# HGRN sample tokens as weights in four 32-column array tiles, states as moving operand, turned back by a selection product

## The chip, the cores and the metric

The kernel runs on one core of one Trainium2 chip. The metric is device time in microseconds (us). The kernel before takes 1646.91 us, the median of three runs (1646.46 to 1647.82).

The names used for engines: PE is TensorE, the matmul array, and PEld its weight loads; DVE is VectorE, ACT ScalarE, POOL GpSimd, and SP SyncE, which here only issues DMAs.

## The reference, cut to what matters

One layer of a hybrid decoder runs on 256 prompt tokens and on 64 sample tokens (8 sequences of 8 tokens). The input projection feeds three groups: RWKV-7 (12 heads), HGRN2 (6 heads, each with a 128 x 128 state) and RG-LRU. Then come an output projection and a gated MLP. The change is in HGRN2:

```python
def step(S, inp):
    q_c, k_c, v_c, lf_c = inp
    b = jnp.cumsum(lf_c, axis=1)
    o_inter = jnp.einsum('bthk,bhkv->bthv', q_c * jnp.exp(b), S)
    dec = jnp.exp(jnp.where(causal, b[:, :, None] - b[:, None, :], -jnp.inf))
    A = jnp.einsum('bthk,btshk,bshk->btsh', q_c, dec, k_c)
    o = o_inter + jnp.einsum('btsh,bshv->bthv', A, v_c)
    ...
    return S, o
...
o = rms_norm(o, lp['hgrn_norm_w'].reshape(HGRN_HEADS, HGRN_HEAD_DIM)).reshape(B, T, HGRN_WIDTH)
o = o * jax.nn.silu(g.astype(f32))
```

For a sample sequence, `o_inter` is the product of its 8 tokens (query times `exp(b)`) with that sequence's own state `S`. There are 8 such states in a head.

## The kernel before

All 320 tokens stand as columns, features on partitions. Weights are streamed in chunks of 512 KB (`raw`, three buffers, a DMA on SP's queue at L167). Each chunk is split into a rounded part `wh` (ACT, L173) and the rest `wl` (DVE, L174). A chunk then is 24 matmuls of 320 moving columns: L198 and L199 in turn, eight of each, with `wh`, and then eight L205 with `wl`. This weight stream is nearly the whole of PE's work.

Everything else runs in chains, which are Python generators. Each chain yields a delay (`L_EV`, `L_SUB` and others); a clock counts weight matmuls and chain steps, and after every four L198/L199 pairs, and after a chunk, the chains that are due go on by a step. The Tile scheduler then makes the final order of each engine from the recorded instructions, and may move them further. The order is so set by these delays and the scheduler together.

In the first third of the kernel six pairs of RWKV heads and six HGRN heads alternate. Two places matter here.

*The inverse triangles of an RWKV pair.* A block of coefficients `mt1` is stored to memory by SP (L568, `dn`) and read back as 16 x 16 blocks (L569, `n16`). Fifteen steps of two DVE operations (L573 and L575) build their inverses `u16`. SP stores them (L576, `du`) and reads them as a whole (L577, `Us`). On PE, L648 transposes `Us`; ACT copies the result (L649), and L665 and what follows merge the triangles into larger ones. The chain has `yield L_SUB` ahead of L648.

*The output of an HGRN head.* L960 to L962 make the prompt's output from `vt` (values with tokens on partitions) and `at` (the attention matrix). L963 makes the sample tokens' part inside a sequence, with 64 rows. L965 runs eight matmuls: the weights are a state `s0` (128 x 128, called `hs` in the trace), and 8 columns of `eb` (query times `exp(b)`) move. The sum's square goes through a matmul with ones (L971), and ACT and DVE make the normalised output from it (L973 to L977). L990/L991 and L998 make the new states, which L1000 adds on DVE.

Of the kernel before, what the change touches and what calls it, by code (L numbers as in the profile page):

```python
# [10 lines left out]
F32 = mybir.dt.float32  # L11
F32R = mybir.dt.float32r
U8 = mybir.dt.uint8
AF = mybir.ActivationFunctionType
ALU = mybir.AluOpType
AX = mybir.AxisListType

P = 128
D = 2048
NK = D // P  # L20
TP = 256
SB, ST = 8, 8
TS = SB * ST
T = TP + TS
# [28 lines left out]
_n = 0  # L53
for _name, _w in (
    ("ident", 128), ("ones", 128), ("bones", 128), ("bswap", 128), 
    ("psw", 128), ("eye2", 64), ("bmx", 4), ("bm4", 4),
):
    CST[_name] = (_n, _w)
    _n += _w
# [7 lines left out]
def kernel(ctx: ExitStack, tc: tile.TileContext, i: dict, o: dict):  # L67
    nc = tc.nc
    V, S, G, PE, SY = nc.vector, nc.scalar, nc.gpsimd, nc.tensor, nc.sync
# [7 lines left out]
    def aux_r():  # L77
        return aux_p.tile([P, 512], F32, tag="aux_r", name="aux_r", bufs=NAUX_R)

    def aux_h():  # L80
        return aux_p.tile([P, 512], F32, tag="aux_h", name="aux_h", bufs=6 - NAUX_R)
# [107 lines left out]
    def gemm(pieces, xh, xl, k0=0, first=True, last=True, ps=None):  # L189
        if ps is None:  # L190
            ps = acc_p.tile([P, 512], F32, tag="acc", name="acc")
        for c, kc in enumerate(pieces):
            prefetch()
            wh, wl = splits.pop(state["used"])
            state["used"] += 1
            for k in range(kc):
                st = first and c == 0 and k == 0
                PE.matmul(ps[:, :T], wh[:, k, :], xh[k0 + k], start=st, stop=False)  # L198
                PE.matmul(ps[:, :T], wh[:, k, :], xl[k0 + k], start=False, stop=False)  # L199
                state["clock"] += 2 * GEMM_COST  # L200
                if k % 4 == 3:
                    tick()
            for k in range(kc):
                en = last and c == len(pieces) - 1 and k == kc - 1
                PE.matmul(ps[:, :T], wl[:, k, :], xh[k0 + k], start=False, stop=en)  # L205
                state["clock"] += GEMM_COST
            k0 += kc
            prefetch()
            tick()
        return ps  # L210
# [9 lines left out]
    def split_tiles(k):  # L220
        return (xp.tile([P, T], F32R, tag=f"xh{k}", name=f"xh{k}"),
                xp.tile([P, T], F32R, tag=f"xl{k}", name=f"xl{k}"))
# [18 lines left out]
    mp = mix.enter_context(tc.tile_pool(name="mixconst", bufs=1))  # L241
    rp = mix.enter_context(tc.tile_pool(name="mixrot", bufs=1))
# [25 lines left out]
    for k in range(NK):  # L268
        if k % 4 == 0:
            split_weights(2 * (k // 8), slice(k % 8, k % 8 + 4))  # L270
        a, b = split_tiles(k)
# [52 lines left out]
    def free(*owners):  # L324
        for owner in owners:
            owner[0] = True

    def ht(name, w=T):
        return rp.tile([P, w], F32, tag="hc", name=name, bufs=BHC)
# [90 lines left out]
    def flat(ap):  # L420
        return ap.rearrange("p a b -> p (a b)")
# [103 lines left out]
    def rwkv_chunks(p, lw, box):  # L525
# [117 lines left out]
        for e in range(2):  # L643
            S.copy(flat(rq[:, 2 * e:2 * e + 2, :]), pss[e][:, 0:256])
        yield L_SUB
        ps = aux_r()
# [175 lines left out]
    def projected(name):  # L822
        ps = gemm(W_CHUNKS, xh, xl)
        t, owner = gt_(name)
        V.tensor_tensor(t, ps[:, :T], rstd, op=ALU.mult)
        return t, owner

    def hgrn_head(n):
        box = {"q": projected("hq")}
        box["f"] = projected("hf")  # L830
        spawn("h", hgrn_steps(n, box))
        box["v"] = projected("hv")
        box["g"] = projected("hg")

    def hgrn_steps(n, box):
        (q, q_own), (f, f_own) = box["q"], box["f"]
        s0 = []
# [4 lines left out]
        b = ht("b", T)  # L842
# [10 lines left out]
        at = ht("at", T)  # L853
# [32 lines left out]
        e, f = ht("e", T), ht("f", T)  # L886
# [13 lines left out]
        while h <= P:  # L900
# [14 lines left out]
            else:  # L915
                ps = aux_h()
# [11 lines left out]
        S.activation(x[:, TP:T], x[:, TP:T], AF.Exp)  # L928
        kd = ht("kd", T)
        V.tensor_tensor(kd, k, x, op=ALU.mult)  # L930
        eb = rp.tile([P, TS], F32, tag="eb", name="eb", bufs=1)
        S.activation(eb, b[:, TP:T], AF.Exp)
        V.tensor_tensor(eb, q[:, TP:T], eb, op=ALU.mult)

        vt = rp.tile([P, 3, P], F32, tag="vt", name="vt", bufs=1)
        kt = rp.tile([P, 3, P], F32, tag="kt", name="kt", bufs=1)
# [6 lines left out]
        for src, t, dst in ((v, both[0], vt), (kd, both[1], kt)):  # L943
            yield L_HG
            ps = aux_h()
# [3 lines left out]
            S.copy(flat(dst), ps[:, 0:3 * P])  # L949

        free(v_own)
        yield L_EV
        free(q_own)
        while "g" not in box:
            yield None
        g, g_own = box["g"]
        S.activation(g, g, AF.Silu)
        yield L_EV
        ps_o = aux_h()
        PE.matmul(ps_o[:, 0:P], vt[:, 0, :], at[:, 0:P], start=True, stop=True)  # L960
        PE.matmul(ps_o[:, P:TP], vt[:, 0, :], a01, start=True, stop=False)
        PE.matmul(ps_o[:, P:TP], vt[:, 1, :], at[:, P:TP], start=False, stop=True)  # L962
        PE.matmul(ps_o[:, TP:T], vt[0:64, 2, :], at[0:64, TP:T], start=True, stop=False, skip_group_check=True)  # L963
        for m in range(SB):
            PE.matmul(ps_o[:, TP + m * ST:TP + (m + 1) * ST], s0[m // 4][:, m % 4, :], eb[:, m * ST:(m + 1) * ST],  # L965
                      start=False, stop=True, skip_group_check=True)
        sq = ht("sqo", T)
        S.activation(sq, ps_o[:, :T], AF.Square)
        yield L_EV
# [19 lines left out]
        ps = aux_h()  # L989
# [195 lines left out]
    for hf in range(2):  # L1185
        hh, hl = [], []
        for jj in range(HJ):
            j = hf * HJ + jj
            ps = gemm(W_CHUNKS, zh, zl)
# [10 lines left out]
            for m in range(1, 3):  # L1200
                V.scalar_tensor_tensor(c[:, 0:N], e[:, m:m + N], pc("fw", 3 * j + m), c[:, 0:N],  # L1201
                                       op0=ALU.mult, op1=ALU.add)
            S.activation(c[:, 0:N], c[:, 0:N], AF.Silu)
            ps = gemm(W_CHUNKS, zh, zl)
# [5 lines left out]
            a = fp.tile([P, T], F32R, tag=f"hh{jj}", name="hh")  # L1210
            b = fp.tile([P, T], F32R, tag=f"hl{jj}", name="hl")
# [6 lines left out]
        for n in range(NK):  # L1218
            ps = gemm(DN_CHUNKS, hh, hl)
# [21 lines left out]
AUX_COST = 0.4  # L1241
L_K = 2.0
L_FRONT = 5.0
L_SUB = 5.0
L_FILL = 1.0
L_EV = 1.5
L_ST = 0.5
# [27 lines left out]
def _constants():  # L1275
    f = np.float32
    r = np.arange(P)
    s, t = r[:, None], r[None, :]
    c = np.zeros((P, NCST), f)

    def put(name, a):
        c[:, CST[name][0]:CST[name][0] + CST[name][1]] = a.reshape(P, -1)

    put("ident", (s == t).astype(f))
    put("ones", np.ones((P, P), f))
    put("bones", (s // 64 == t // 64).astype(f))
    put("bswap", (s // 64 != t // 64).astype(f))
    s6 = (r % 64)[:, None]
    t6 = np.arange(64)[None, :]
    strict, causal = s6 < t6, s6 <= t6  # L1290
    m1 = np.zeros((P, 2, 2, 64), f)
    m2 = np.zeros((P, 2, 2, 64), f)
    for q in range(2):
        on = (r // 64 == q)[:, None]
        for a, cond in enumerate((strict, causal)):
            m1[:, a, q] = on & cond
            m2[:, a, q] = ~on & cond
    same8 = (r % 64 // 8)[:, None] == np.arange(64)[None, :] // 8
    ms = np.zeros((P, 4, 2, 64), f)
    for q in range(2):  # L1300
        on = (r // 64 == q)[:, None]
        ms[:, 0, q], ms[:, 1, q] = on & same8 & strict, on & same8 & causal
        ms[:, 2, q], ms[:, 3, q] = ~on & same8 & strict, ~on & same8 & causal
    put("psw", ((s + 64) % P == t).astype(f))
    put("eye2", (s6 == t6).astype(f))
    put("bm4", ((r % 32 // 8)[:, None] == np.arange(4)[None, :]).astype(f))
    put("bmx", ((r // 8)[:, None] % 8 == 4 * (r // 64)[:, None] + np.arange(4)[None, :]).astype(f))
    m = np.zeros((len(MASKS), P, P), f)
    m[0] = (s // 4 == t // 4) & (s <= t)
    for n, h in enumerate((4, 8, 16, 32, 64)):  # L1310
        m[n + 1] = (s // (2 * h) == t // (2 * h)) & (s % (2 * h) < h) & (t % (2 * h) >= h)
    m[6] = m[3].T
    return c, np.concatenate([m.transpose(1, 0, 2).reshape(P, -1)] + [x.reshape(P, -1) for x in (m1, m2, ms)], axis=1)
# [95 lines left out]
```

## Time and profile before

| | |
|---|---|
| median of three runs | 1646.91 us |
| profiled execution | 1651.69 us |
| its span | 1649.9 us |
| mean granted TensorE clock | 0.992 |
| weight stream L198, L199, L205 (shares of the chain of waits) | 27%, 26%, 27% |
| bytes read from memory | 225.62 MB |

The span is the time from the first to the last instruction of the profiled execution; 1.8 us of the execution lie around it. In the timeline a row shows where a group of instructions starts, how long it lasts, its engine and line, the tiles it writes and reads, and how many instructions (or records) it has. Square brackets hold idle time ahead of it and what ended it. An fp32 matmul of the chains leaves two records, a weight matmul one.

### The profile page before, as it was taken

To read this page: it belongs to the slowest core of one execution; us is meant where nothing else is said; L and a number is where in the kernel's file an instruction comes from. 1 tells how busy PE (TensorE), PEld (TensorE's weight loads), DVE (VectorE), ACT (ScalarE), POOL (GpSimd) and SP (SyncE) were. 2 spreads that over 40 slices of the span, in tenths; PEclk is the share of its full clock that TensorE was granted. 3 is DMA by queue.
4 is the path that set the end of the run, shared out by engine and by line. 5 is a ranking of instruction groups with operands and counts; after the bars stand their busy time and mean duration, and the time that the engine had idled before them with its cause. 6 is when DMAs were issued, how large, how long until landed. Compare 5 with 4: busy or idle time off the path is not lost.

```text
span 1649.9 us, 29024 instructions
## 1 busy us (share of the span) xinstructions
PE 1613.8 (98%) x11508; PEld 1567.1 (95%) x11508; DVE 983.7 (60%) x1952; ACT 827.9 (50%) x1293; POOL 154.8 (9%) x369
## 2 busy tenths in 40 slices
PE   7999999999999999999999999999999999999996
PEld 7888998999899899999999999999999999999996
DVE  7777777877777656555555554343455555554444
ACT  7675767676766874443434433323343343344441
POOL 2001010101012210010000000000000000010000
PEclk9999999999999999999999999999999999999998
DMA  7434443434343455444444544555544444455553
GB/s 255 151 123 123 121 132 113 131 113 131 113 128 120 149 158 165 147 157 154 149 146 152 151 146 144 151 154 151 153 150 146 152 154 151 146 155 153 146 153 105
DMA packets 87103, 238.86 MB, mean 145 GB/s; under 512 B 16568, under 2 KB 30312, under 8 KB 86968
## 3 DMA queue, kind: packets, MB, share of 16 engines
q1 hardware_dynamic: 82072, 221.67, 44.1%
q0 software_dynamic: 4896, 15.35, 2.9%
q8 instruction: 90, 1.47, 0.4%
q14 instruction: 45, 0.37, 0.1%
HBM read 225.62 MB, written 11.37 MB: 144 GB/s over the span
## 4 chain that ended last, share of the span: by engine, by line
PE 90%; DVE 3%; DMA 3%; ACT 3%; issue 1%; SPq 0%; DVEq 0%; ACTq 0%
PE acc L205 27%; PE acc L198 27%; PE acc L199 26%; DMA U<-du 1%; PE aux_r L665 1%; PE aux_h L875 1%; DVE wl L174 1%; PE aux_h L965 1%; DMA xr<-in_xT 1%; DMA du<-u 1%; PE aux_r L198 0%; PE aux_h L998 0%; PE aux_r L199 0%; ACT wh L173 0%; DVE x L1234 0%
## 5 line engine op out<-in xcount | busy, mean ns | idle before, releaser
L173 ACT CAST wh<-raw 128x1024 fp32r<-128x1024 f32 (+2 forms) x412 | 421.1, 1023 | 518.9 <-PE acc L199 315.8
L198 PE MATMUL acc<-xh,wh 128*128 128x320 f32 x2208 | 668.4, 316 | 3.2 <-DVE ext L342 3.2
L199 PE MATMUL acc<-xl,wh 128*128 128x320 f32 x2208 | 658.0, 311 | 0.0
L174 DVE TENSOR_TENSOR wl<-raw,wh 128x1024 fp32r<-128x1024 f32 (+2 forms) x412 | 489.5, 1189 | 238.5 <-ACT wh L173 109.0
L198 PEld LDWEIGHTS acc<-xh,wh 128*128 128x128 f32 x2208 | 416.8, 189 | 10.9 <-issue 7.8
L199 PEld LDWEIGHTS acc<-xl,wh 128*128 128x128 f32 x2208 | 417.4, 189 | 2.1
L205 PE MATMUL acc<-xh,wl 128*128 128x320 f32 x2208 | 382.5, 314 | 0.2 <-DVE wl L174 0.2
L205 PEld LDWEIGHTS acc<-xh,wl 128*128 128x128 f32 x2208 | 337.9, 190 | 4.2 <-issue 1.0
L198 PE MATMUL acc<-hh,wh 128*128 128x320 f32 x704 | 208.2, 311 | 0.0
L199 PE MATMUL acc<-hl,wh 128*128 128x320 f32 x704 | 207.9, 308 | 0.0
L198 PEld LDWEIGHTS acc<-hh,wh 128*128 128x128 f32 x704 | 132.4, 188 | 0.0
L199 PEld LDWEIGHTS acc<-hl,wh 128*128 128x128 f32 x704 | 132.2, 188 | 0.0
L205 PE MATMUL acc<-hh,wl 128*128 128x320 f32 x704 | 118.9, 309 | 0.0
L1196 POOL COPY ncch<-fe 128x18 f32<-128x18 f32 x44 | 49.6, 1127 | 653.4 <-DVE fe L1195 653.4
L205 PEld LDWEIGHTS acc<-hh,wl 128*128 128x128 f32 x704 | 107.1, 188 | 0.0
L1206 DVE TENSOR_TENSOR fv<-acc,rstd 128x320 f32<-128x320 f32 x44 | 21.6, 492 | 98.1 <-PE acc L205 98.1
L1194 DVE TENSOR_TENSOR fe<-acc,rstd 128x256 f32<-128x256 f32 x44 | 18.7, 425 | 99.2 <-PE acc L205 99.2
L214 ACT CAST hh<-fv 128x320 fp32r<-128x320 f32 x44 | 20.3, 461 | 96.9 <-DVE fv L1208 96.9
L198 PE MATMUL acc<-yhl,wh 128*128 128x320 f32 x224 | 66.2, 310 | 0.5 <-ACT yhl L214 0.5
L199 PE MATMUL acc<-yhl,wh 128*128 128x320 f32 x224 | 66.2, 309 | 0.0
L1201 DVE SCALAR_TENSOR_TENSOR fc<-fe,prm,fc 128x336 f32<-128x336 f32 x88 | 49.8, 565 | 1.6
L1199 ACT ACTIVATE fc<-fe,prm 128x336 f32<-128x336 f32 x44 | 29.5, 669 | 35.1 <-DVE fe L1195 35.1
(406 smaller groups left out, 1650.5 us busy)
## 6 DMA issues: line engine op xcount, KB each, us to landing
raw<-in_w_up SPq DMA_DIRECT2D x176, 512.0 KB, 3.5
raw<-in_w_in SPq DMA_DIRECT2D x100, 512.0 KB, 3.7
raw<-in_w_dn SPq DMA_DIRECT2D x64, 512.0 KB, 3.6
raw<-in_w_out SPq DMA_DIRECT2D x32, 512.0 KB, 3.8
raw<-in_w_dn SPq DMA_DIRECT2D x32, 384.0 KB, 3.4
out_s_hgrn<-hs POOLq DMA_DIRECT2D x12, 256.0 KB, 3.8
hs<-in_hs POOLq DMA_DIRECT2D x10, 256.0 KB, 3.8
x<-in_xT POOLq DMA_DIRECT2D x16, 160.0 KB, 2.8
```

The costliest lines, as they stand in the source:

```text
L173: S.copy(wh[:, ks, :], raws[n][:, ks, :])
L174: V.tensor_tensor(wl[:, ks, :], raws[n][:, ks, :], wh[:, ks, :].bitcast(F32), op=ALU.subtract)
L198: PE.matmul(ps[:, :T], wh[:, k, :], xh[k0 + k], start=st, stop=False)
L199: PE.matmul(ps[:, :T], wh[:, k, :], xl[k0 + k], start=False, stop=False)
L205: PE.matmul(ps[:, :T], wl[:, k, :], xh[k0 + k], start=False, stop=en)
L214: S.copy(xh, src)
L665: PE.matmul(ps[q, b * 64:(b + 1) * 64], lhs[q, b, q], r[q], start=True, stop=True)
L1194: V.tensor_tensor(e[:, 2:258], ps[:, 0:TP], rstd[:, 0:TP], op=ALU.mult)
L1196: G.tensor_copy(ncch[:, j], e[:, 248:EX].rearrange("p (b s) -> p b s", s=10)[:, :, 8:10])
L1199: S.activation(c[:, 0:N], e[:, 0:N], AF.Identity, scale=pc("fw", 3 * j), bias=pc("fb", j))
L1201: V.scalar_tensor_tensor(c[:, 0:N], e[:, m:m + N], pc("fw", 3 * j + m), c[:, 0:N], op0=ALU.mult, op1=ALU.add)
L1206: V.tensor_tensor(val, ps[:, :T], rstd, op=ALU.mult)
```

## The change

The product of the sample tokens with their states is turned round. `eb` becomes a tile of 128 x 4 x 32, made once and filled with zeros once. A head writes its 64 tokens into the first 16 of each 32 columns, so that two sequences share a group of 32. Four matmuls take these groups as weights, each in its own 32 columns of the array, and move the two states of the group (256 columns). The result has tokens on partitions, 32 to a group, and for each token both states' products side by side. Two DVE operations with a constant mask (`bm2`) keep the right one in `oi`, which holds zeros in the unused rows. One matmul with `oi` as weights and a constant selection matrix (`sel`, 128 x 64) then adds it to the output with features on partitions. The matmul ahead of it takes all 128 rows of `vt` and `at` instead of 64. The new block stands in a step of its own, ahead of the wait for the gate `g`, so the chain has one more `yield L_EV`. `L_SUB` goes from 5.0 to 6.5. L960 to L963 become L973 to L976, L971 becomes L982, L990/L991 L1001/L1002, L998 L1009, L1000 L1011, and L871 L875.

```diff
     ("ident", 128), ("ones", 128), ("bones", 128), ("bswap", 128), 
-    ("psw", 128), ("eye2", 64), ("bmx", 4), ("bm4", 4),
+    ("psw", 128), ("eye2", 64), ("bmx", 4), ("bm4", 4), ("sel", 64), ("bm2", 2),
...
+    eb = mp.tile([P, 4, 32], F32, tag="eb", name="eb")
+    G.memset(eb, 0.0)
...
-        eb = rp.tile([P, TS], F32, tag="eb", name="eb", bufs=1)
-        S.activation(eb, b[:, TP:T], AF.Exp)
-        V.tensor_tensor(eb, q[:, TP:T], eb, op=ALU.mult)
+        ev = eb[:, :, 0:16]
+        S.activation(ev, b[:, TP:T].rearrange("p (g s) -> p g s", s=16), AF.Exp)
+        V.tensor_tensor(ev, q[:, TP:T].rearrange("p (g s) -> p g s", s=16), ev, op=ALU.mult)
...
+        free(q_own)
         yield L_EV
-        free(q_own)
+
+        ps = aux_h()
+        for g in range(4):
+            PE.matmul(ps[32 * g:32 * g + 32, 0:TP], eb[:, g, :],
+                      s0[g // 2][:, 2 * (g % 2):2 * (g % 2) + 2, :].rearrange("p a b -> p (a b)"), start=True, stop=True)
+        oi = rp.tile([P, P], F32, tag="oi", name="oi", bufs=1)
+        V.tensor_scalar(oi, ps[:, 0:P], cc("bm2")[:, 0:1], None, op0=ALU.mult)
+        V.scalar_tensor_tensor(oi, ps[:, P:TP], cc("bm2")[:, 1:2], oi, op0=ALU.mult, op1=ALU.add)
+        yield L_EV
         while "g" not in box:
...
-        PE.matmul(ps_o[:, TP:T], vt[0:64, 2, :], at[0:64, TP:T], start=True, stop=False, skip_group_check=True)
-        for m in range(SB):
-            PE.matmul(ps_o[:, TP + m * ST:TP + (m + 1) * ST], s0[m // 4][:, m % 4, :], eb[:, m * ST:(m + 1) * ST],
-                      start=False, stop=True, skip_group_check=True)
+        PE.matmul(ps_o[:, TP:T], vt[:, 2, :], at[:, TP:T], start=True, stop=False, skip_group_check=True)
+        PE.matmul(ps_o[:, TP:T], oi, cc("sel"), start=False, stop=True, skip_group_check=True)
...
-L_SUB = 5.0
+L_SUB = 6.5
...
+    put("sel", ((r // 32 * 16 + r % 32)[:, None] == np.arange(64)[None, :]).astype(f) * (r % 32 < 16)[:, None])
+    put("bm2", (r // 8 % 4)[:, None] == np.arange(2)[None, :])
```

The instruction order of each engine shows what else moves. First PE's row of instructions at the output of head 0, before (operands stand as output, moving or stationary tiles, and columns; `x4` counts equal rows):

```order
L198 MATMUL acc<-xh_151,wh 128x320
L199 MATMUL acc<-xl_152,wh 128x320
L960 MATMUL aux_h<-at,vt 128x128
L961 MATMUL aux_h<-a_1207,vt 128x128
L962 MATMUL aux_h<-at,vt 128x128
L963 MATMUL aux_h<-at,vt 128x64
L965 MATMUL aux_h<-eb,hs_1036 128x8 x4
L965 MATMUL aux_h<-eb,hs_1038 128x8 x4
L198 MATMUL acc<-xh_161,wh 128x320
L199 MATMUL acc<-xl_162,wh 128x320
```

The same place in the changed kernel has the new block first, and the output some 32 weight matmuls behind it:

```order
L198 MATMUL acc<-xh_217,wh 128x320
L199 MATMUL acc<-xl_218,wh 128x320
L804 MATMUL aux_r<-sg,lw 128x320
L961 MATMUL aux_h<-hs_1038,eb 32x256 x2
L961 MATMUL aux_h<-hs_1040,eb 32x256 x2
L205 MATMUL acc<-xh_183,wl 128x320
...
L205 MATMUL acc<-xh_173,wl 128x320
L973 MATMUL aux_h<-at,vt 128x128
L974 MATMUL aux_h<-a_1209,vt 128x128
L975 MATMUL aux_h<-at,vt 128x128
L976 MATMUL aux_h<-at,vt 128x64
L977 MATMUL aux_h<-cst,oi 128x64
L198 MATMUL acc<-xh_183,wh 128x320
```

The eight small matmuls are gone, and the head's output stands 16 weight matmuls later than it did.

Next PE's row around L648 of the second pair (tiles `U` are the inverse triangles, `cst` the identity), before:

```order
L198 MATMUL acc<-xh_217,wh 128x320
L199 MATMUL acc<-xl_218,wh 128x320
L871 MATMUL aux_h<-e,f 128x128
L205 MATMUL acc<-xh_183,wl 128x320
L648 MATMUL aux_r<-cst,U 128x128 x4
L871 MATMUL aux_h<-e,f 128x128
L205 MATMUL acc<-xh_187,wl 128x320
L205 MATMUL acc<-xh_191,wl 128x320
```

And in the changed kernel:

```order
L198 MATMUL acc<-xh_173,wh 128x320
L199 MATMUL acc<-xl_174,wh 128x320
L205 MATMUL acc<-xh_139,wl 128x320
L205 MATMUL acc<-xh_143,wl 128x320
L648 MATMUL aux_r<-cst,U 128x128 x4
L205 MATMUL acc<-xh_147,wl 128x320
L205 MATMUL acc<-xh_151,wl 128x320
```

L648 stands 23 weight matmuls earlier (the 738th instead of the 761st), behind the second L205 of the chunk ahead of the one before. The pairs behind it show the same shift; the first pair shows none.

Last SP's queue at the same place (`raw` the weight chunks, `dn` and `n` the coefficients on their way out and back, `du` and `U` the inverses), before:

```order
L167 DMA raw<-in_w_in 128x1024 x8
L568 DMA dn_245<-mt_1807 128x5x128
L167 DMA raw<-in_w_in 128x1024
L569 DMA n_1832<-dn_245 40x16x16
L167 DMA raw<-in_w_in 128x1024 x3
L576 DMA du_246<-u_1833 40x16x16
L167 DMA raw<-in_w_in 128x1024
L577 DMA U<-du_246 128x5x128
L167 DMA raw<-in_w_in 128x1024 x9
```

And in the changed kernel:

```order
L167 DMA raw<-in_w_in 128x1024 x8
L568 DMA dn_245<-mt_1796 128x5x128
L569 DMA n_1821<-dn_245 40x16x16
L167 DMA raw<-in_w_in 128x1024 x3
L576 DMA du_246<-u_1822 40x16x16
L167 DMA raw<-in_w_in 128x1024
L577 DMA U<-du_246 128x5x128
L167 DMA raw<-in_w_in 128x1024 x10
```

The weight load between L568 and L569 is gone from there, so L576 stands one weight load earlier in the queue. On DVE the cast L174 that stood ahead of the last step of L573/L575 stands behind it now, and the two L1011 (L1000 before) stand inside the fifteen steps instead of ahead of them.

## The prediction

> **What bounds the kernel now.** I read the page's busy times first, then its chain, then TensorE's waits.
>
> ```profile
> PE 1613.8 (98%) x11508; PEld 1567.1 (95%) x11508; DVE 983.7 (60%) x1952; ACT 827.9 (50%) x1293; POOL 154.8 (9%) x369
> PE 90%; DVE 3%; DMA 3%; ACT 3%; issue 1%; SPq 0%; DVEq 0%; ACTq 0%
> PE aux_r L648 <- DMA U<-du: 5.6, 6, 1.3
> ```
>
> TensorE (PE) is busy 98% of the span and holds 90% of the chain. So only three things can move the time: what PE has to do, what PE waits for, and the clock it is granted. One wait is touched by the change: the six transposes of L648 wait 5.6 us in all for the inverse triangles (U), which come back from memory at L577.
>
> The clock is seen in windows; the columns are us, PE busy, PEld, DVE, ACT, POOL, granted clock, DMA share, GB/s. The second fence has the same windows with L965 alone (us, PE, PEld, clock, DMA, GB/s).
>
> ```profile
> 46.28:49.69 3.41, 1.99 (x7) 2.02 (x8) 3.00 (x6) 2.13 (x4) 0.19 (x1) 0.50 0.08 28
> 302.28:305.70 3.42, 3.42 (x24) 3.26 (x24) 2.24 (x5) 2.24 (x3) 1.11 (x2) 1.00 0.51 155
> 384.20:387.61 3.41, 3.41 (x15) 3.21 (x13) 0.95 (x2) 2.33 (x2) 0.65 (x1) 0.50 0.43 151
> 548.04:551.45 3.41, 3.41 (x15) 3.21 (x13) 0.12 (x1) 2.47 (x3) 0.00 (x0) 0.50 0.47 180
> ```
> ```profile
> 298.87:302.28 3.41, 1.66 (x15) 1.66 (x15) 1.00 0.50 153
> 380.79:384.20 3.41, 1.95 (x16) 1.86 (x16) 1.00 0.49 159
> ```
>
> The clock is set per stretch of 3.41 us. Behind a stretch that holds all 16 records of an 8-column block (380.79) the next runs at 0.50; behind one that holds 15 (298.87) it doesn't. That happens three times (384.20 the first, 548.04 the last), each time directly behind such a block. A stretch mostly without work does it too: 46.28 follows PE's wait for the first layer's data. So what counts is how long few columns stream: some 1.8 us inside one stretch. At half the clock half of 3.41 us is lost: 1.7 us.
>
> **The change, part A: the block of small matmuls.** Head 0 in PE's timeline (start, length, line, operand shapes, records), with rows of two neighbours:
>
> ```profile
> 137.20 0.39 PE L961 MATMUL aux_h<-a,vt 128*128 128x128 f32 x2
> 137.42 0.39 PE L962 MATMUL aux_h<-at,vt 128*128 128x128 f32 x2
> 137.74 0.43 PE L963 MATMUL aux_h<-at,vt 64*128 64x64 f32 x2
> 138.10 1.95 PE L965 MATMUL aux_h<-eb,hs 128*128 128x8 f32 x16
> 139.91 0.39 PE L198 MATMUL acc<-xh,wh 128*128 128x320 f32 x1
> ```
> ```profile
> 229.39 0.66 PE L583 MATMUL aux_r<-cst,xs 128*64 128x128 f32 x8
> 229.97 0.49 PE L990 MATMUL aux_h<-vt,kt 128*128 128x128 f32 x2
> 237.70 1.03 PE L618 MATMUL aux_r<-s,ARs 128*128 128x256 f32 x4
> ```
>
> An fp32 matmul leaves two records; L961 to L962 gives 0.11 us for a record. L962's two records end at 137.64, the next weight matmul starts at 139.91: L963 and L965 take 2.27 us. After the change two plain matmuls (L976 and L977, 64 columns each, four records, at most 4 x 0.11 = 0.44) stand there: 1.83 us are saved in a head. The new block is four matmuls of 256 columns, eight records. L618 gives a record of 256 columns (1.03 less its last one's 0.38, over three) 0.22. Do four tiles of 32 columns run beside each other? L583's eight records of 128 columns go into two halves of 64 columns: one after another they would take 8 x 0.11 = 0.88, and they take 229.97 - 229.39 = 0.58, switches included; so tiles overlap here. Bounds: 2 x 0.22 = 0.44 with nothing around it, and 8 x 0.22 plus a switch, 0.2, = 1.97 one after another. I take 0.44 and about 0.27 for going in and out of tiles (L583: 0.58 - 0.44 = 0.14 for the overlapped case; twice that, as four weights must be loaded), 0.72. Saved: 1.83 - 0.72 = 1.11 in a head, times 6: **-6.7 us**; bounds -8.3 and +0.8.
>
> [...]
>
> VectorE gets two masked adds a head (128 wide, well under L1000's 0.65 below) and GpSimd one memset. VectorE is 60% busy, GpSimd 9%; what waits for the adds is L977, 32 weight matmuls (32 x 0.147 = 4.7 us, part B) behind: nothing. If that cover went, it would be six times about a microsecond. The head's end moves 16 weight matmuls later; its output is read only by the output projection, far behind.
>
> **Part B: the wait at L648.** A chunk is sixteen L198/L199 matmuls and then eight L205. By the rows of the order above, L648 stood behind the first L205 of a chunk, and now stands behind the second L205 of the chunk ahead of that one. All that is queued behind L648 on PE is the weight stream, so its wait lies on the path. Pair 2 before, on PE, on SyncE's queue, in the list of DMA issues (last column: us to landing) and on VectorE:
>
> ```profile
> 142.33 0.70 PE L971 MATMUL aux_h<-sqo,cst 128*128 128x320 f32 x2
> 142.63 0.55 PE L198 MATMUL acc<-xh,wh 128*128 128x320 f32 x1
> 143.02 0.31 PE L199 MATMUL acc<-xl,wh 128*128 128x320 f32 x1
> ...
> 251.91 1.34 PE L205 MATMUL acc<-xh,wl 128*128 128x320 f32 x8
> 255.57 0.39 PE L205 MATMUL acc<-xh,wl 128*128 128x320 f32 x1
> 257.22 0.63 PE L648 MATMUL aux_r<-cst,U 128*128 128x128 f32 x4 [1.26 <-DMA U<-du]
> ```
> ```profile
> 236.57 12.43 SPq L167 DMA_DIRECT2D raw<-in_w_in  x3
> 249.10 0.32 SPq L576 DMA_DIRECT2D du<-u  x1
> 251.41 0.33 SPq L167 DMA_DIRECT2D raw<-in_w_in  x1
> 253.12 0.38 SPq L577 DMA_DIRECT2D U<-du  x1
> ```
> ```profile
> raw<-in_w_in SPq DMA_DIRECT2D x100, 512.0 KB, 3.7
> dn<-mt SPq DMA_DIRECT2D x6, 320.0 KB, 2.5
> U<-du SPq DMA_DIRECT2D x6, 320.0 KB, 3.6
> ```
> ```profile
> 235.32 1.23 DVE L174 TENSOR_TENSOR wl<-raw,wh 128x1024 fp32r<-128x1024 f32 x1 [2.29 <-ACT bkt L604]
> 236.53 1.29 DVE L1000 TENSOR_TENSOR hs<-aux_h,hs 128x512 f32<-128x512 f32 x2
> 237.74 0.16 DVE L573 TENSOR_TENSOR t<-n,u 40x15 f32<-40x15 f32 x1
> ...
> 247.42 1.23 DVE L174 TENSOR_TENSOR wl<-raw,wh 128x1024 fp32r<-128x1024 f32 x1
> 248.56 0.16 DVE L573 TENSOR_TENSOR t<-n,u 40x15 f32<-40x15 f32 x1
> 248.76 0.17 DVE L575 TENSOR_TENSOR u<-u,t 40x15 f32<-40x15 f32 x1
> ```
>
> *When PE comes.* A weight matmul takes (1.34 - 0.31) / 7 = 0.147 us. Before, PE is ready at 255.57 + 0.147 = 255.72 and starts at 257.22, a wait of 1.50. After, L648 stands behind the second of the eight L205: 251.91 + 2 x 0.147 = 252.20. The normalisation matmul (L971, now L982) moved ahead of it and brings 143.02 - 0.147 - 142.33 = 0.54: 252.74, that is 2.98 earlier.
>
> *When U comes.* Three things pull it forward. The chain L573/L575 begins where L1000 began, 236.53 + 0.54 (the same shift) = 237.07 instead of 237.74. The cast L174 that held its last step (248.56 - 247.42 = 1.14, where a step takes about 0.2) goes, and the two L1011 (1.29) come in between instead: together near +0.2. So the chain ends near 248.3 and L576 leaves at 248.4 rather than 249.10. The third is the largest: before, a raw load of 512 KB left just ahead of L576 on the same queue, and du's 40 KB were there only at 253.12, 4.02 after issue; after, no raw load is ahead. dn, the other store of this kind and of eight times the bytes, lands in 2.5. By that L577 leaves at 250.9; U takes 257.22 - 253.12 = 4.1 as now (a raw load goes ahead of it in both): 255.0, 2.2 earlier. If du takes 4.0 still, only the 0.7 remain.
>
> So the wait grows by 2.98 - 2.2 = 0.76 a pair. Pairs 1 to 5 show the same shift by 23 matmuls, pair 0 none: 5 x 0.76 = **+3.8 us**; bounds 0 (U as much earlier as PE) and 5 x 2.98 = +14.9 (U not earlier).
>
> **Part C: clock behind the longer waits.** The five waits were about 1.3 from start to start, and are then about 2.1, above the 1.8 that lowers the clock when they fall into one stretch. Of 3.41 us of positions a wait of 2.1 has 1.8 in one stretch in some 2.0, three of five: 3 x 1.7 = **+5.1**; bounds 0 and +8.5.
>
> **Part D: clock behind the old block.** The eight-column block goes and streams 256 columns instead, so the three slow stretches behind it go: **-5.1**; bound 0, if the timed runs had none.
>
> L_SUB's 5.0 to 6.5 I price at nothing: the order shows L648 earlier, not later, since the head's moved steps decide its place.
>
> Sum: -6.7 + 3.8 + 5.1 - 5.1 = -2.9. On the profile's own time of 1651.69 that is 1648.8; the median of the runs shown is 4.8 lower, so 1646.91 - 2.9 = **1644.0**.
>
> **The rivals.**
>
> *Slower: U doesn't follow.* The store du is slow by its 16-element pieces, not by the load ahead, and takes 4.0 still. Then U is 0.7 earlier, the wait grows by 2.28: 5 x 2.28 = 11.4, all five stretches behind fall to half (+8.5): -6.7 + 11.4 + 8.5 - 5.1 = +8.1, 1655.0 (1658.5 if U doesn't move). For it: du carries 40 KB in 4.02 where 320 KB take 2.5. Against: the raw load's 3.7 explains that by itself. With three slow stretches it turns from gain to loss where U comes less than 1.64 earlier.
>
> *The tiles run one after another.* Block 1.97: +0.8 instead of -6.7, 1651.5. Against it L583.
>
> *No slow stretches behind the waits.* Idle time of 2 us does not lower the clock, only small matmuls do: -6.7 + 3.8 - 5.1 = -8.0, 1638.9. For it: none of the six waits shown, up to 1.5, has a slow stretch behind it. Against: 46.28 stands behind an idle stretch, though a longer one.
>
> [...]
>
> *U comes as much earlier as PE.* The waits stay and C goes: -6.7 - 5.1 = -11.8, 1635.1. For it: U's chain has slack in its other steps; against: 2.98 is more than all I found.
>
> **How the numbers follow.** Forecast 0.40; U late 0.20; tiles serial 0.10; no slow stretches 0.17; U early 0.13. About 0.2%, 3.3 us, is what a measurement can tell from no change: 1643.6 to 1650.2. The forecast lies at its edge and gives 0.19 faster, 0.20 same, 0.01 slower; U late 0.03 same, 0.17 slower; tiles serial 0.04 and 0.06; no slow stretches 0.15 faster, 0.02 same; U early 0.13 faster. Together 0.47 faster, 0.29 same, 0.24 slower. The range leaves out the worst half of "U late" and little of the early cases: 1634 to 1656. The forecast's own range is 1641 to 1647.
>
> **What would show it.** In the profile after: L961's eight records in 0.6 to 0.8 us (A); L648's wait for U near 1.8 a time in five pairs, du landing 2.5 after L576, L577 without a load ahead of du (B); 0.50 stretches behind about three of these waits and none behind a head (C, D). L961 near 2 us, waits of 3 us or more, or L977 waiting for VectorE would make the prediction wrong.

## The result and the profile after

The changed kernel takes 1663.53 us (median of four runs, 1661.09 to 1665.05) beside 1647.37 for the kernel before (four runs, 1646.46 to 1651.71). The ratio is 1.009, with a 95% interval from 1.0078 to 1.0102: about 16 us slower, above the range that was given. The profiled execution took 1664.05 us, its span 1662.3.

The page's busy times, its chain by engine, and three rows of TensorE's waits (us in all, times, longest):

```profile
PE 1611.5 (97%) x11472; PEld 1555.1 (94%) x11472; DVE 987.8 (59%) x1964; ACT 829.9 (50%) x1295; POOL 150.0 (9%) x370
PE 80%; DVE 9%; ACT 5%; DMA 4%; issue 2%; SPq 0%; DVEq 0%; ACTq 0%
PE aux_r L648 <- DMA U<-du: 15.5, 5, 3.8
PE aux_r L787 <- DVE y L772: 3.8, 4, 1.0
PE aux_h L1074 <- DVE oi L965: 1.2, 1, 1.2
```

PE is busy 2.3 us less than before, and the span is 12.4 longer: the time went into waiting. L648 waits 9.9 us more than before; L787, which waited 0.7, waits 3.1 more. L1074, a matmul of RG-LRU, waits once for the new adds on DVE. The chain shows it too: PE's share falls from 90% to 80%, and DVE and ACT, which feed the late inputs, stand in its place.

The new block does what was expected of it. PE's timeline at head 0:

```profile
132.22 0.64 PE L961 MATMUL aux_h<-hs,eb 128*32 128x256 f32 x8
132.79 1.44 PE L205 MATMUL acc<-xh,wl 128*128 128x320 f32 x8
134.07 0.31 PE L198 MATMUL acc<-xh,wh 128*128 128x320 f32 x1
...
138.25 0.33 PE L976 MATMUL aux_h<-at,vt 128*128 128x64 f32 x2
138.42 0.39 PE L977 MATMUL aux_h<-cst,oi 128*128 128x64 f32 x2
138.62 0.39 PE L198 MATMUL acc<-xh,wh 128*128 128x320 f32 x1
138.85 0.31 PE L199 MATMUL acc<-xl,wh 128*128 128x320 f32 x1
```

The block takes 132.79 - 132.22 = 0.57 and 0.10 of the way out (from 132.79 to 134.07 stand 1.28, eight matmuls take 1.18). L976 and L977 take 0.37.

And pair 2 at L648, on PE and on SyncE's queue:

```profile
250.33 0.46 PE L205 MATMUL acc<-xh,wl 128*128 128x320 f32 x2
254.57 1.09 PE L648 MATMUL aux_r<-cst,U 128*128 128x128 f32 x4 [3.78 <-DMA U<-du]
```
```profile
246.04 0.30 SPq L576 DMA_DIRECT2D du<-u  x1
247.16 0.33 SPq L167 DMA_DIRECT2D raw<-in_w_in  x1
249.27 0.38 SPq L577 DMA_DIRECT2D U<-du  x1
249.84 0.38 SPq L167 DMA_DIRECT2D raw<-in_w_in  x1
```

The store du is there 3.2 us after issue (249.27 - 246.04; it was 4.0), and U is used 5.3 after issue (254.57 - 249.27; it was 4.1). The raw load that no longer stands ahead of du leaves 1.1 us behind it, and a further one 0.6 us behind U. What the store gained, the load lost, and over pairs 1 to 5 as well: du took 3.3 on average where it took 4.1, and U 4.5 where it took 3.8.

The windows of the waits of pairs 2 and 3 (us, PE busy, PEld, DVE, ACT, POOL, granted clock, DMA share, GB/s):

```profile
251.00:254.41 3.41, 0.00 (x0) 0.00 (x0) 0.95 (x3) 0.57 (x1) 0.00 (x0) 1.00 0.61 215
254.41:257.82 3.41, 3.25 (x22) 2.96 (x24) 0.47 (x1) 1.05 (x3) 0.00 (x0) 0.50 0.01 6
336.30:339.70 3.40, 0.43 (x3) 0.16 (x2) 1.36 (x4) 1.22 (x2) 0.17 (x1) 1.00 0.74 253
339.70:343.10 3.40, 3.30 (x22) 3.00 (x24) 0.52 (x1) 1.05 (x3) 0.00 (x0) 0.50 0.01 6
```

Behind these two stretches, with 3.41 and 2.97 us without PE's work, the next ran at 0.50. The same holds at pair 4, where two stretches in a row ran at 0.50 (425.06 to 431.88); the waits of pairs 1 and 5 (2.50 and 2.42 us), which lie across two stretches with at most 1.5 us in one, had 1.00 behind them. No head is followed by a slow stretch any more.

### The profile page after: what moved, and what is told of

It is laid out like the page before. It is cut to its first block, busy times and chain, and to the rows that moved or that the text cites. A ratio compares the mean times of both kernels' runs of the same rounds, so it can differ in the third digit from the quotient of the medians.

```text
span 1662.3 us, 28976 instructions
## 1 busy us (share of the span) xinstructions
PE 1611.5 (97%) x11472; PEld 1555.1 (94%) x11472; DVE 987.8 (59%) x1964; ACT 829.9 (50%) x1295; POOL 150.0 (9%) x370
## 4 chain that ended last, share of the span: by engine, by line
PE 80%; DVE 9%; ACT 5%; DMA 4%; issue 2%; SPq 0%; DVEq 0%; ACTq 0%
PE acc L198 24%; PE acc L205 24%; PE acc L199 24%; DVE wl L174 2%; DMA U<-du 1%; PE aux_r L665 1%; DMA du<-u 1%; ACT wh L173 1%; DVE u L575 1%; DVE t L573 1%; PE aux_h L879 1%; DMA xr<-in_xT 0%; PE aux_r L198 0%; PE aux_r L205 0%; PE aux_r L199 0%
## 5 line engine op out<-in xcount | busy, mean ns | idle before, releaser
L174 DVE TENSOR_TENSOR wl<-raw,wh 128x1024 fp32r<-128x1024 f32 (+2 forms) x412 | 489.6, 1190 | 244.7 <-PE acc L205 112.5
L205 PE MATMUL acc<-xh,wl 128*128 128x320 f32 x2208 | 382.5, 314 | 0.3 <-DVE wl L174 0.2
L205 PEld LDWEIGHTS acc<-xh,wl 128*128 128x128 f32 x2208 | 336.4, 189 | 8.7 <-issue 6.3
L205 PE MATMUL acc<-hh,wl 128*128 128x320 f32 x704 | 118.8, 308 | 0.0
L205 PEld LDWEIGHTS acc<-hh,wl 128*128 128x128 f32 x704 | 107.1, 187 | 0.0
```

Source lines behind the costliest of these rows:

```text
L174: V.tensor_tensor(wl[:, ks, :], raws[n][:, ks, :], wh[:, ks, :].bitcast(F32), op=ALU.subtract)
```

## The experiments

Three theories stood. S: the extra step of the HGRN chain moves L648 and the store of U, and the loss is a wait. P: the new product costs by itself. L: L_SUB makes the loss. Each of the four runs that follow does or undoes some of these parts; the places of L648 are those of the instruction order. Each run has its own runs of the kernel before beside it (medians 1648.04 to 1649.48), and the ratios and the words "above" and "below" refer to those.

**New product without the step of its own.** The changed kernel with these two lines changed; the block then runs in the step ahead of the gate.

```diff
         V.scalar_tensor_tensor(oi, ps[:, P:TP], cc("bm2")[:, 1:2], oi, op0=ALU.mult, op1=ALU.add)
-        yield L_EV
         while "g" not in box:
...
-L_SUB = 6.5
+L_SUB = 5.0
```

> New product, but the extra yield of the chain is taken out and L_SUB is 5.0 again: the instruction order then puts L648 back at the 761st weight matmul and SP's queue as before. Theory S (the extra step moves L648 and U's store, the loss is a wait): L648's waits stay near 5.6 us in all, a head gains 1.3 us (block and output 1.7 instead of 3.0), 6 x 1.3 = 7.8: 1639.6 us, down to 1634 if the three half-clock stretches behind the old block go as well. Theory P (the new product itself costs: its adds on DVE, a PSUM buffer held longer): about 1660 us, L648's waits unchanged. Theory L (L_SUB makes the loss): as S, about 1640.

Measured: 1643.75 us, ratio 0.9965 (0.9952 to 0.9979). L648 waits 6.6 us in all, and no stretch runs at half clock between the first 60 us and the last 15. S and L hold as far as the direction goes; P falls. The gain is smaller than S said, since a new wait stands in this kernel:

```profile
PE aux_r L648 <- DMA U<-du: 6.6, 6, 1.7
PE aux_h L976 <- DVE oi L965: 2.6, 6, 0.5
```

With 16 weight matmuls between the block and the output the adds on DVE are not covered.

**Old product with the step.** The changed kernel with the block and the adds taken out, L_SUB 5.0, and the eight matmuls back in the output:

```diff
-        PE.matmul(ps_o[:, TP:T], oi, cc("sel"), start=False, stop=True, skip_group_check=True)
+        for m in range(SB):
+            PE.matmul(ps_o[:, TP + m * ST:TP + (m + 1) * ST], s0[m // 4][:, m % 4, :], eb[:, m // 2, m % 2 * ST:(m % 2 + 1) * ST],
+                      start=False, stop=True, skip_group_check=True)
```

> The eight 8-column matmuls of before, but with the extra yield of the changed kernel (an empty step) and L_SUB 5.0: L648 stands at the 738th weight matmul, the head's output later. Theory S: L648's waits are near 15.5 us in all as in the changed kernel, +10, and some stretches at half clock follow: 1657 to 1662 us. Theory P and theory L: 1647 us, the waits near 5.6.

Measured: 1666.4 us, ratio 1.0095 (1.0067 to 1.0123), with four runs from 1658.33 to 1668.83. The new block, its adds and the selection are not in it (the padded `eb` and the 128 rows of L976 are), and it is as slow as the changed kernel. An empty step in the chain is enough. The profiled run took 1658.33 at a mean granted clock of 0.993; the other three have 0.989 to 0.990, so its waits show less than what the median lost:

```profile
PE aux_r L648 <- DMA U<-du: 12.4, 6, 3.4
```

**L_SUB alone, on either kernel.** First the changed kernel with `L_SUB = 5.0`:

> The changed kernel with L_SUB 5.0 alone undone: L648 stays at the 738th weight matmul, the steps behind it stand 8 weight matmuls earlier. Theory S: L648 waits 15.5 us in all as in the changed kernel, only L787's waits for y (3.8 us) go back to 0.7: about 1660 us. Theory P: 1663 us. Theory L: about 1640 us.

Measured: 1658.43 us, ratio 1.0051 (1.0033 to 1.0069): 9.0 above its kernel before, where the changed kernel is 16.2 above, so L_SUB makes some 7 of the 16. L787 waits 0.7 again, and L648:

```profile
PE aux_r L648 <- DMA U<-du: 13.2, 6, 3.8
```

Then the kernel before with `L_SUB = 6.5`:

> The kernel before with L_SUB 6.5 alone: L648 stays at the 761st weight matmul, the steps behind the triangles stand 8 weight matmuls later. Theory S: only L787's waits for y appear (+3 us): 1650 us, L648's waits 5.6. Theory P: 1647 us. Theory L: about 1660 us.

Measured: 1657.1 us, ratio 1.0048 (1.0033 to 1.0062). Its waits:

```profile
PE aux_r L648 <- DMA U<-du: 6.4, 5, 2.1
PE aux_r L787 <- DVE y L772: 3.8, 4, 1.0
```

So neither S nor L holds alone. L_SUB costs 6 to 8 us without moving L648. L787's waits are the same 3.8 as in the changed kernel, and that is 3.1 of it. L875, L743 and L648 together wait 2.9 us more than in the kernel before; the remaining 1.6 are open. The steps behind L648 come 8 weight matmuls later, and DVE's last operations for y (L756 and L772) then stand behind work of the next pair (L474 to L497).

**The step, with L648 back in its place.** This is the cleanest cut between "the step costs" and "the place of L648 costs". The changed kernel with L_SUB 5.0 and the step's delay shortened:

```diff
         V.scalar_tensor_tensor(oi, ps[:, P:TP], cc("bm2")[:, 1:2], oi, op0=ALU.mult, op1=ALU.add)
-        yield L_EV
+        yield 0.5
```

> The changed kernel with L_SUB 5.0, whose extra step yields 0.5 instead of 1.5. It keeps the step of its own; the order puts L648 back at the 761st weight matmul, and the head's output 8 weight matmuls earlier than in the changed kernel. Theory S (where L648 stands is what costs): L648's waits 5.6 to 6.6 us in all, no half-clock stretch behind them, time 0.995 to 0.998 of before, 1641 to 1645 us. Rival (the extra step itself, its later output and its separate visits of PE, costs): as with L_SUB 5.0 alone, 1.005 of before.

Measured: 1641.35 us, ratio 0.9957 (0.9942 to 0.9972); no half-clock stretch behind the waits.

```profile
PE aux_r L648 <- DMA U<-du: 5.8, 6, 1.4
```

One number, 1.5 to 0.5, takes some 16 us off (9.0 above the kernel before becomes 7.1 below). In the profiled runs L648 waits 7.4 us less and three stretches at half clock are gone, some 5.1 us; the spans differ by 12.3. Beside L648's place the number also moves the head's output by 8 weight matmuls, and a raw load on SyncE's queue (1.2 us ahead of du instead of 3.2). So this run shows what the delay costs, and the waits name L648; it doesn't move L648 alone.

**The block in kd's step**, which is the fastest kernel found. L_SUB is 5.0, there is no extra step, and the block stands in the loop that transposes v and kd:

```diff
             yield L_HG
+            if src is kd:
+                ps = aux_h()
+                for g in range(4):
+                    PE.matmul(ps[32 * g:32 * g + 32, 0:TP], eb[:, g, :],
...
             ps = aux_h()
             for m in range(2):
```

> The new product with no step of its own and L_SUB 5.0, its four matmuls in the step that transposes kd, some 32 weight matmuls ahead of the output. L648 at the 761st. Theory S: as the kernel without the extra step, and its 2.6 us of waits for oi go: 0.995 of before, 1641 us. Rival (the adds hold DVE and delay others by as much): 1644 us.

Measured: 1638.74 us (1638.37 to 1639.25), ratio 0.9942 (0.9927 to 0.9957). The waits for oi are gone.

**One tile instead of four.** The same kernel, but each of the four matmuls takes all of `eb` as weights. It leaves out the separation of the groups: a token gets the sum of their products.

```diff
-                    PE.matmul(ps[32 * g:32 * g + 32, 0:TP], eb[:, g, :],
-                              s0[g // 2][:, 2 * (g % 2):2 * (g % 2) + 2, :].rearrange("p a b -> p (a b)"), start=True, stop=True)
+                    PE.matmul(ps[:, 0:TP], flat(eb),
+                              s0[g // 2][:, 2 * (g % 2):2 * (g % 2) + 2, :].rearrange("p a b -> p (a b)"), start=g == 0, stop=g == 3)
```

> As the kernel with the block in kd's step, but all 128 columns of eb are the weights in each of the four matmuls, which add into one tile: it computes the sum of the four groups' products instead of each group's own, and cannot use column tiles. If the four column tiles run beside each other: the block takes 8 x 0.21 = 1.7 us instead of about 0.6, and the kernel is 6 x 1.1 = 6.6 us slower, 1648. [...]

Measured: 1644.92 us, 6.2 more than with four tiles. The block in PE's timeline, with four tiles and then with one:

```profile
129.58 0.64 PE L952 MATMUL aux_h<-hs,eb 128*32 128x256 f32 x8
130.15 0.44 PE L959 MATMUL aux_h<-cst,kd 128*128 128x128 f32 x2
```
```profile
129.45 1.89 PE L952 MATMUL aux_h<-hs,eb 128*128 128x256 f32 x8
131.17 0.38 PE L959 MATMUL aux_h<-cst,kd 128*128 128x128 f32 x2
```

It took 0.57 or 1.72: the tiles ran beside each other. Six times 1.15 is 6.9, close to the 6.2 measured.

**L648 later.** Two kernels try to remove its waits. The first is the kernel with the block in kd's step, with `L_SUB = 14.0` and two delays of the merging steps at 0:

> As the kernel with the block in kd's step, with L_SUB 14.0 and two yields of the merging steps at 0: the order puts L648 at the 776th weight matmul (15 behind before), L787 where it was. Theory S: 15 weight matmuls are 2.2 us, more than any of the waits of 1 to 2 us, so L648's waits go (6 us) and L787 waits as before: 0.991 of before, 1635 us. Rival (the steps behind L648 now wait for each other, for ACT's and DVE's copies): 1641 us or more.

Measured: 1646.16 us, ratio 0.9983 (0.9974 to 0.9992), 7.4 more than the kernel it was made from. L648 waits for nothing, and three other places do:

```profile
PE aux_h L879 <- DVE at L880: 4.6, 5, 1.9
PE aux_h L960 <- POOL both L945: 3.1, 4, 0.8
PE aux_r L446 <- DMA lw<-in_lw: 2.5, 2, 1.9
```

The rival was right about the size, though the waits are those of the next head's steps. The second is the changed kernel with `L_SUB = 11.5`:

> The changed kernel with L_SUB 11.5: L648 stands at the 760th weight matmul (22 later than in the changed kernel, one ahead of before), with L665 and what follows 24 to 40 later than in the changed kernel. Theory S: L648's waits fall from 15.5 to 4 to 7 us in all, no half-clock stretch behind them. If nothing else waits, 1643 us (0.997); rival (the steps behind it, moved later, meet the next head's and pair's work and wait there, as L787 did for 8 matmuls): L648's waits fall but others of about the same size appear, 1650 us or more.

Measured: 1654.64 us, ratio 1.0044 (1.0029 to 1.0059). Again the waits move on:

```profile
PE aux_r L760 <- DVE gbd L728: 11.2, 4, 2.8
PE aux_r L648 <- DMA U<-du: 0.6, 1, 0.6
```

**U on another queue.** The changed kernel with L_SUB 5.0 and U's load on GpSimd's queue:

```diff
-        SY.dma_start(out=Us, in_=whole(d_u))
+        G.dma_start(out=Us, in_=whole(d_u))
```

> The changed kernel with L_SUB 5.0, and U's load (L577) on GpSimd's queue instead of SyncE's. GpSimd waits for du's landing there anyway, ahead of its memset at L565. L648 stays at the 738th weight matmul. Theory Q (U shares SyncE's queue with the raw load behind or ahead of it, and that makes it 3.2 to 5.3 us): U takes about 3 us, L648's waits fall from 13.2 to about 8 us in all, 1653 us (1.002 of before). Rival (the transfers share the 16 DMA engines, whatever their queue): U takes 4 us and more as before, waits 13 us, 1658 us.

Measured: 1670.67 us, ratio 1.0141 (1.012 to 1.0162). U takes longer, not shorter: PE uses it 4.9 to 5.6 us after issue, where it was 3.2 to 5.3. GpSimd's timeline at pair 2, then the list of DMA issues (KB, median us to landing), then PE's waits:

```profile
255.36 0.86 POOL L577 DMA_DIRECT2D U<-du  x1 [6.14 <-DMA du<-u]
```
```profile
U<-du POOLq DMA_DIRECT2D x6, 320.0 KB, 5.0
```
```profile
PE aux_r L648 <- DMA U<-du: 24.5, 6, 4.8
```

Taking U off SyncE's queue did not make it faster. The issue on GpSimd takes 0.86 where SyncE's takes 0.38, so the run doesn't show whether the shared DMA engines or the other queue's own cost hold it. As a dose it is useful. With the new product and L_SUB 5.0 throughout, L648's waits of 5.8, 13.2 and 24.5 us in all go with 1641, 1658 and 1671 us.

## Why the prediction was wrong, step by step

Two steps failed: B put the growth of the wait at L648 at 3.8 us where it is 9.9, and L_SUB was put at nothing where it costs some 7.

**A, the block (predicted -6.7): right.** 0.67 were measured for the block (0.72 predicted, way out included) and 0.37 for L976 and L977 (at most 0.44). The kernel with four tiles against one shows that the overlap was rightly read from L583: the four took 0.57, and without the tiles the same eight records took 1.72 (the bound of 1.97 held 0.2 for a switch, the author's estimate). The four tiles share their 128 rows (128*32 in the trace), and they ran beside each other.

**B, the wait at L648 (predicted +3.8): failed, in the size of a term.** The direction and the place were right: PE came earlier and waited for U. From the chain's end to PE's arrival the prediction had 252.74 - 248.3 = 4.4 us. In the trace it is about 4.7: PE is ready at 250.33 + 2 x 0.147 = 250.62, and L576 leaves at 246.04, which is 0.1 behind the chain's end. The two transfers were mis-sized. "By that L577 leaves at 250.9" set du at dn's 2.5, and U "4.1 as now"; pair 2 shows 3.2 and 5.3. That makes 1.9 more for pair 2, a wait of 3.9 instead of 2.3, and 9.9 more over all pairs instead of 3.8. Over pairs 1 to 5 du and U took 7.85 us on average where the prediction had 2.5 + 4.1 = 6.6; five times this 1.25 is 6.2, the whole of the difference. The removed raw load did shorten du, from 4.0 to 3.2, as it should if it was in the way. The prediction did not follow it to its new place, 1.1 us behind du. In the run with L_SUB 11.5 the loads stand otherwise, and du is there at 2.1 (L576 at 245.78, L577 at 247.89):

```profile
245.78 0.30 SPq L576 DMA_DIRECT2D du<-u  x1
247.47 0.33 SPq L167 DMA_DIRECT2D raw<-in_w_in  x1
247.89 0.39 SPq L577 DMA_DIRECT2D U<-du  x1
```

So du's time goes with the places of the raw loads, and its small pieces alone do not set it. Why U took 5.3 in pairs 2 and 4 and about 4 in 1, 3 and 5 stays open.

**C, half clock behind the waits (predicted three of five, +5.1): right in kind, and the count in part by luck.** Pairs 2, 3 and 4 have them, pair 4 two in a row, so 4 x 1.7 = 6.8. Three of five was worked out for waits of 2.1 us, and the waits were 2.4 to 3.8. The rival without such stretches is refuted: 251.00 holds no matmul at all and 336.30 hardly any, and 0.50 follows each; in the run with U on GpSimd's queue it follows the waits of all pairs but the first. In the changed kernel waits of 3.1 to 3.8 us were followed by 0.50, and those of 2.4 and 2.5, each across two stretches, were not; in the old product with the step, at L_SUB 5.0, 1.87 us inside one stretch was enough (last section).

**D, no half clock behind the heads (predicted -5.1): right for the profiled execution, too much for the median.** None is there in the changed kernel, nor in the other kernels with four tiles. From the profiled kernel before to the block in kd's step the span falls by 12.4 us, where A and D had 11.8. By the medians it is 9.7: the 19 runs of the kernel before beside that kernel have mean granted clocks from 0.991 (1652.72 us) to 0.995 (1645.66 us), and the profiled one has 0.992 at 1651.69 us. The six of them from 1646 to 1648 us, near the prediction's 1646.91, have 0.994 or 0.995, so they hold fewer stretches at half clock than the three that the prediction took off this median.

**L_SUB (predicted nothing): failed.** "The order shows L648 earlier, not later" was true, and the argument stopped there. The steps behind L648 do move by 8 weight matmuls, and L787 then waits for y. L_SUB costs some 7 us in the changed kernel and a ratio of 1.0048 in the kernel before.

The parts by run, by medians and each against its own kernel before:

| part | predicted | measured |
|---|---|---|
| new product, L648 in place (A, D) | -11.8 | -7.1 |
| the step at its full delay (B, C) | +8.9 | +16.1 |
| L_SUB 6.5 | 0 | +7.2 |
| sum | -2.9 | +16.2 |

Each measured part is the difference of one kernel to the next, so their sum is the whole by construction. In the profiled runs the step's part shows as 7.4 us more at L648 and three stretches at half clock (5.1), and L_SUB's as 3.1 more at L787, 2.3 more at L648 and one such stretch (1.7).

The rival "U doesn't follow", 8.1 to 11.6 us above the kernel before, came nearest, and with L_SUB undone the 9.0 lie inside it. Its reason was not the one that held: du did get faster, and U got slower by nearly as much. The two together took 8.5 us in pair 2 (3.2 + 5.3), where they had taken 8.1 (4.0 + 4.1).

That "the head's moved steps decide its place" was half of it: what moves L648 is not the new product but the delay of one step. The old product with that step has L648 at the same 738th weight matmul, and a delay of 0.5 brings it back.

## What to carry to other kernels

Where a list scheduler places work by its own estimates, an edit's price lies in what it moves: undo the move and keep the edit before judging the edit. Here the product gains 0.4% to 0.6%, and one delay beside it loses about 1%. A transfer taken out of one place in a queue must be followed to its new place, since the transfer that the path waits for may come later for it (here the store went from 4.1 to 3.3 us on average, and U from 3.8 to 4.5). And a wait is best removed with what stands behind it in view: two kernels that removed it, or nearly so, paid elsewhere.

## What was not expected of the hardware

**Half the clock followed a gap of 1.87 us.** Idle time is what PE busy lacks of a stretch of 3.41 us in the windows. The first two rows are of the old product with the step (1.87 us idle, and 0.50 behind it), the other two of the run with U on GpSimd's queue (1.83 us idle, and 1.00 behind it):

```profile
170.08:173.49 3.41, 1.54 (x12) 1.38 (x14) 0.00 (x0) 0.88 (x3) 0.00 (x0) 1.00 0.34 134
173.49:176.91 3.42, 3.42 (x42) 2.97 (x44) 2.44 (x6) 1.31 (x6) 0.00 (x0) 0.50 0.33 80
425.27:428.68 3.41, 1.58 (x11) 1.32 (x9) 2.11 (x5) 2.36 (x6) 1.47 (x4) 1.00 0.76 259
428.68:432.10 3.42, 0.88 (x7) 0.91 (x8) 0.00 (x0) 0.21 (x1) 0.00 (x0) 1.00 0.26 101
```

Over the kernels run here, between 65 and 1600 us, each stretch with 1.87 us or more of idle time was followed by one at 0.50 (17 stretches, 15 of them idle at L648, one at L446 and one at L760). Stretches with 1.83 or less were not, apart from two kinds: those with an eight-column block, and one at pair 4 of the changed kernel, which had 0.69 us of idle time and was itself at half clock; why stays open. Behind the eight-column block of the old product the clock fell as well: where 1.82 us or more of it lay inside one stretch, 0.50 followed (six times; 1.82, 1.95 and 1.95 in the kernel before), and where it was 1.78 or less, it never did (twelve times; at most 1.66 in the kernel before). A longer wait went free: pair 1 of the changed kernel waited 2.5 us, at most 1.5 of it in one stretch.

**A store of 64-byte pieces took up to twice as long beside the loads.** The 40 KB of du took from 2.1 to 4.3 us from its issue to that of U on the same queue. It was 4.0 to 4.3 with a raw load issued 0.4 us ahead, 3.2 to 3.4 with one 1.2 ahead and one 2.1 behind, 2.7 to 3.7 with one 3.2 ahead and one 1.1 behind, and 2.1 to 2.7 with one 4.4 ahead and one 1.7 behind. The loads ahead and behind moved together, so which of them counts is not shown.
